# Rows of four later modulation vectors summed on TensorE, three row tiles side by side in column groups

## The chip, the cores and the metric

The kernel runs on one core of one Trainium2 chip. The metric is the device time of one execution in microseconds. Three executions of the kernel before took 723.62, 726.33 and 727.22 us, so its median is 726.33 us. One more execution was taken with the hardware profiler, and every row shown below is from that one.

## The reference

The reference is a decoder trunk of two layers over one sequence of 512 positions and 1024 features. Each layer draws a shift, a scale and a gate from one conditioning vector and computes, in float32:

```python
cond = jax.nn.silu(c)                                   # (1, 1024)
for layer in range(2):
    shift, scale, gate = jnp.split(cond @ w_ada[layer] + b_ada[layer], 3, axis=-1)
    h = x * (1.0 + scale[:, None, :]) + shift[:, None, :]
    y = _even_mixer(h, ...) if layer % 2 == 0 else _odd_mixer(h, ...)
    x = _layer_norm(ALPHA * x + (1.0 + gate[:, None, :]) * y, ln_g[layer], ln_b[layer])
```

The even mixer is one input projection, block-sparse attention over eight heads, sliding-window attention over eight more, a gate and an output projection. The odd mixer is a sparse attention with an indexer and a stick-breaking attention. What the change touches is the product of `cond` with `w_ada` alone: a vector of 1024 times a matrix of 1024 by 1024, once for each of the six pieces (shift, scale and gate of two layers).

## The kernel before, in words

Shift and scale of the first layer are needed at once and are made in `start` by `ada_chunk` (line 519), which is not changed. The other four pieces are "later": the gate of layer 0 and the scale, shift and gate of layer 1. Each is a matrix of 1024 by 1024, that is eight row tiles of 128 rows (index `k`), each in two halves of 512 columns (index `c`). `ada_rows` (line 436) makes 16 steps of a piece, one for each `k` and `c`. A step fetches 128 rows by 512 columns (256 KB) through SyncE's queue into a buffer with the tag `arow` (three buffers while the pool `tmp0` is open, two afterwards), and adds the rows, each multiplied by its element of `cond`, into a tile `accr` of 128 by 1024. On VectorE that is one instruction; on GpSimd it is a multiplication on ScalarE (line 461) and an addition in two halves on GpSimd (line 68, in the helper `Pieces`). The gate of layer 0 gives its first half to VectorE and its second to GpSimd; scale and shift of layer 1 the other way round; the gate of layer 1 gives both to GpSimd. When all rows are in, `column` (line 480) adds up the 128 partitions of `accr` with eight matmuls against a column of ones, and `finish` adds the bias.

Where these steps stand is set by `weave`. It takes a list of attention units, one a turn, spreads the projection's matmuls (`fill`) between their stages, and puts the next of the `side` steps behind every turn. TensorE runs in exactly this written order. The order of the queues of VectorE, ScalarE, GpSimd and SyncE is made by a planner from its own estimate of the times, and each of them works strictly in its order. The side steps go to:

- `attend(0)`, 16 units: six empty steps, then the 21 steps of the gate of layer 0 (16 rows, four empty, one column step);
- `attend(1)`, 16 units: the scale of layer 1 (16 rows, six empty, one column step) and the first half of the shift's rows, 31 steps;
- the first six window units: the remaining 15 steps of the shift, and one of `out_split`;
- the six empty units behind the last window, in which the output projection runs: the 16 row steps of the gate of layer 1. Its column step follows after the first projections of layer 1.

Two constants come from `constants` (line 159): `condr`, which is `cond` repeated 32 times for each `k` (128 by 8 by 32), and `third`, a column with a one in the partitions 0, 32 and 64 and zeros elsewhere. `ada_chunk` uses both: its function `shift` multiplies four row tiles of 256 columns by `condr` on TensorE (line 548), where row tile `k` goes to output partitions `32 * (k % 3)` and up, so that three matmuls write different groups of 32 columns of the array; `third` then adds the three groups.

Of the kernel before, what the change touches and what calls it, by code (L numbers as in the profile page):

```python
# [9 lines left out]
F32 = mybir.dt.float32  # L10
F32R = mybir.dt.float32r
BF = mybir.dt.bfloat16
AF = mybir.ActivationFunctionType
OP = mybir.AluOpType
# [5 lines left out]
DM = 1024  # L20
KT = 8
# [55 lines left out]
class Trunk:  # L77
# [84 lines left out]
    def constants(self):  # L162
        nc, sb, a = self.nc, self.base, self.a
        crow = self.t("rx")[0:8, 0:128]
        nc.sync.dma_start(crow, a["c"].rearrange("o (k p) -> (o k) p", p=128))
        self.ident = sb.tile([128, 128], F32, name="ident")
        nc.sync.dma_start(self.ident, a["k_ident"])
        self.rot = sb.tile([128, 128], F32, name="rot")
        self.ones = sb.tile([128, 128], F32, name="ones")
        nc.vector.memset(self.ones, 1.0)  # L170
        self.eps = sb.tile([128, 1], F32, name="eps")
        nc.vector.memset(self.eps, EPS)
        ps = self.psum("pv", "colc")
        nc.tensor.transpose(ps[:, 0:8], crow, self.ident[0:8, 0:8])
        cc = self.sm("cc", 8)
        nc.vector.tensor_copy(cc, ps[:, 0:8])
        th = self.sm("cth", 8)
        nc.scalar.activation(th, cc, AF.Tanh, scale=0.5)
        nc.vector.tensor_scalar(th, th, 0.5, 0.5, op0=OP.mult, op1=OP.add)
        self.cond = sb.tile([128, 8], F32, name="cond")  # L180
        nc.vector.tensor_tensor(self.cond, th, cc, op=OP.mult)
        self.condr = self.t("r1")[:, 0:256].rearrange("p (k m) -> p k m", m=32)
        nc.vector.tensor_copy(self.condr, self.cond[:, :, None].to_broadcast([128, 8, 32]))
        self.third = self.tmp.tile([128, 1], F32, name="third")
        nc.vector.memset(self.third, 0.0)
        for j in range(3):
            nc.vector.memset(self.third[32 * j:32 * j + 1], 1.0)
# [245 lines left out]
        nc.vector.tensor_tensor(v[:, j, :, 64:128], p4, f32(v[:, j, :, 0:64]), op=OP.subtract)  # L433


    def ada_rows(self, l, part, engines):

        nc = self.nc
        box = {}
        per = 4 if "tmp1" in self.pools else 1  # L440

        def step(k, c):
            cc = slice(512 * c, 512 * c + 512)
            if k % per == 0:
                if per == 1:
                    r = self.ada_row("wr").rearrange("p (a n) -> p a n", a=1)
                else:
                    r = self.base.tile([128, 4, 512], F32, tag="raw", name="wr", bufs=2)
                src = self.a["w_ada"][l][128 * k:128 * (k + per), part * DM + 512 * c:part * DM + 512 * c + 512]
                nc.sync.dma_start(r, src.rearrange("(k p) n -> p k n", p=128))  # L450
                box["r"] = r
                if k + c == 0:
                    box["acc"] = self.base.tile([128, DM], F32, tag="accr", name=f"accr{l}{part}")
            acc, r = box["acc"], box["r"][:, k % per]
            w = self.cond[:, k:k + 1]
            eng = engines[c]
            if eng is self.gp:
                if k == 0:
                    nc.scalar.activation(acc[:, cc], r, AF.Copy, scale=w)
                else:  # L460
                    nc.scalar.activation(r, r, AF.Copy, scale=w)  # L461
                    eng.tensor_tensor(acc[:, cc], acc[:, cc], r, op=OP.add)
            elif k == 0:
                eng.tensor_scalar(acc[:, cc], r, w, None, op0=OP.mult)
            else:
                eng.scalar_tensor_tensor(acc[:, cc], r, w, acc[:, cc], op0=OP.mult, op1=OP.add)  # L466
        steps = [lambda k=k + j, c=c: step(k, c) for k in range(0, KT, per) for c in range(2) for j in range(per)]
        return steps, lambda: box["acc"]

    def ada_row(self, name):  # L470
        return self.tmp.tile([128, 512], F32, tag="arow", name=name, bufs=3 if "tmp0" in self.pools else 2)

    def ada_cols(self, l, parts, engines=None, late=6):


        nc = self.nc
        names = ("shift", "scale", "gate")
        dst = {p: self.base.tile([128, 8], F32, name=f"{names[p]}{l}") for p in parts}

        def column(part, acc, k):  # L480
            if k == 0:
                dst["ps"] = self.psum("pv", f"adac{l}{part}")
            nc.tensor.matmul(dst["ps"][:, k:k + 1], acc[:, k * 128:k * 128 + 128], self.ones[:, 0:1], start=True, stop=True)

        def finish(part):
            ps = dst.pop("ps")
            b0 = 8 + 24 * l + 8 * part
            nc.vector.scalar_tensor_tensor(dst[part], ps[:, 0:8], float(part > 0), self.cols[:, b0:b0 + 8],
                                           op0=OP.add, op1=OP.add)
            if part == 2:  # L490
                nc.vector.tensor_scalar(dst[part], dst[part], 0.5, None, op0=OP.mult)
        steps = []
        for p in parts:
            st, acc = self.ada_rows(l, p, engines or [self.E(z) for z in {0: 'vg', 1: 'gv'}[l]])
            steps += st + [lambda: None] * late
            steps.append(lambda p=p, acc=acc: ([column(p, acc(), k) for k in range(KT)], finish(p)) and None)
        return steps, dst

# [544 lines left out]
    def even_mixer(self, side, more):  # L1043

        nc, W = self.nc, self.a["w_in_even"][0]
# [44 lines left out]
        def bv_turn():  # L1090
            pt = self.psum("pt", "bvT", (128, 4, 128))
            for j in range(QT):
# [6 lines left out]

        fill = [*rotated("aq1", 256, "q1", 0.125, raw), *rotated("ak1", 768, "k1", 1.0), *self.values(W, 1280, "av1", keep("v1")),  # L1100
                self.col_tile(wkv, 0, "bk", bk), self.col_tile(wkv, 1, "bv", bv)]
        self.weave(attend(0), fill, [lambda: None] * 6 + side)
        bq0 = rotated("bq0", 1536, "bq0", 0.125)
        fill = [bq0[0], self.part(bv_turn, 0.43), bq0[1], *rotated("bq1", 1792, "bq1", 0.125), *self.gates(W, 2304, 2, osum[2]),
                *self.gates(W, 2304, 3, osum[3])]
# [340 lines left out]
    def run(self):  # L1446
# [7 lines left out]
        self.at = self.pool("at0")  # L1454
        self.tmp = self.pool("tmp0")
        self.constants()
        side, gate = self.ada_cols(0, (2,), late=4)
        more, ada1 = self.ada_cols(1, (1, 0), late=6)
        steps = side + more
        n0, n1, n2 = 21, 52, 69  # L1460
        osum, window = self.even_mixer(steps[:n0], steps[n0:n1])
        self.close("tmp0")
        self.tmp = self.pool("out0")
        W = self.a["w_in_even"][0]
# [9 lines left out]
        windows = [window(i, g) for i in range(QT) for g in range(2)]  # L1474
        us, box = {}, {}
        o = [f() for f in osum]
        rest = steps[n1:n2]
        self.weave(windows[:6], fill, rest + [lambda: None] * max(0, 5 - len(rest)) + [lambda: self.out_split(0, o, box, (0,))])
        G = to_all()
        self.weave(windows[6:7], [], [lambda n=n: self.out_split(0, o, box, (n,)) for n in (1, 2, 3)])  # L1480

# [11 lines left out]
        fill = self.out_half(0, 0, box, G, resid, done)  # L1493
        self.weave(windows[7:] + [None] * 2, fill[:6])
        self.out_split(1, o, box)
        side, gate1 = self.ada_cols(1, (2,), [self.E(z) for z in 'gg'], 0)
        self.weave([None] * 6, fill[6:], steps[n2:] + side[:-1])
        modulation()
        self.close("qk0")
        h1 = self.pool("h1", side="right")  # L1500
# [23 lines left out]
        first = firsts(halves[0], {})  # L1524
        t = turn(2)
        self.run_parts(*first[2:], self.between(first[0], t[:4]), self.between(first[1], t[4:]))
        for f in side[-1]() or []:
            f()
        self.close("out0", "at0", "h0")

        self.qk_pool = self.pool("x1", side="right")
# [36 lines left out]
        box = {}  # L1568
# [80 lines left out]
```

## Time and profile before

| | kernel before |
|---|---|
| median of three executions | 726.33 us |
| profiled execution | 727.53 us |
| its span, first to last instruction | 725.0 us |
| TensorE matmul (PE) busy | 667.3 us, 92% |
| TensorE weight load (PEld) busy | 539.5 us, 74% |
| VectorE (DVE) busy | 512.7 us, 71% |
| GpSimd (POOL) busy | 381.3 us, 53% |
| ScalarE (ACT) busy | 377.7 us, 52% |
| mean granted TensorE clock | 0.960 |

The profiled execution took 727.53 us, 2.5 us more than its span; it lies 1.2 us above the median of the runs shown. Busy time is the union of an engine's instructions. Matmuls overlap each other in the array, so what TensorE can still take on is better read from the distance between the starts of its instructions than from the busy share. The granted clock is 1 at 2.4 GHz and 0.5 at 1.2 GHz. An "idle before" in square brackets is time in which the engine had nothing to do, with what ended it.

### The profile page before, as it was taken

The numbers are of one execution on the slowest core, as the hardware profiler recorded it, in microseconds if no ns is written. First come the engines' busy times: TensorE is split into PE (matmuls) and PEld (weight loads), VectorE is DVE, ScalarE is ACT, GpSimd is POOL, SyncE is SP. The second block draws the span as 40 slices with busy tenths as digits, with TensorE's granted clock in tenths as the row PEclk, the third lists the DMA queues.
The fourth block names the chain that finished last, engine by engine and source line by source line (L and its number), as shares of the span: only waits on it lengthen the run. The fifth ranks groups of instructions, "written<-read, shape, count | busy, mean of one in ns | idle before, by whom it ended". The sixth has DMA issues, their size and how long they took to land.

```text
span 725.0 us, 11339 instructions
## 1 busy us (share of the span) xinstructions
PE 667.3 (92%) x3866; PEld 539.5 (74%) x3866; DVE 512.7 (71%) x1157; ACT 377.7 (52%) x820; POOL 381.3 (53%) x492
## 2 busy tenths in 40 slices
PE   3799989998999999999999999899999987888994
PEld 1566758875777777799987768687767866777994
DVE  3646376566656888977753269999948979567787
ACT  2225266566555566766523453656656447376630
POOL 1456584135514544696855644445677276361743
PEclk9899999999999998899999999989999999898998
DMA  8991552135315711348443212211167686243231
GB/s 259 345 315 60 175 165 84 55 99 165 117 59 189 258 62 58 106 106 286 149 140 101 73 59 74 62 56 54 34 172 189 169 283 202 67 149 124 86 119 58
DMA packets 82643, 97.55 MB, mean 135 GB/s; under 512 B 8697, under 2 KB 66906, under 8 KB 82586
## 3 DMA queue, kind: packets, MB, share of 16 engines
q1 hardware_dynamic: 82586, 96.84, 43.2%
q8 instruction: 30, 0.49, 0.3%
q14 instruction: 27, 0.22, 0.1%
HBM read 86.32 MB, written 10.49 MB: 134 GB/s over the span
## 4 chain that ended last, share of the span: by engine, by line
PE 55%; DVE 13%; DMA 11%; POOL 10%; ACT 4%; issue 4%; SPq 2%; POOLq 0%; DVEq 0%; ACTq 0%
DMA wr<-in_w_ada 5%; PE gp L306 4%; PE gp L308 4%; PE gp L307 4%; PE s L788 3%; PE pt L712 3%; DMA x<-in_x 2%; PE pv L738 2%; DMA kc<-knh 2%; PE pv L737 2%; PE s L1003 1%; POOL u L68 1%; PE rot L620 1%; POOL accr L68 1%; PE dq L306 1%
## 5 line engine op out<-in xcount | busy, mean ns | idle before, releaser
L68 POOL TENSOR_TENSOR accr<-accr,wr 128x256 f32<-128x256 f32 x70 | 57.6, 846 | 48.8 <-ACT wr L461 45.8
L306 PE MATMUL gp<-hh,gh 128*128 128x512 f32 x128 | 56.9, 445 | 0.0
L714 DVE TENSOR_TENSOR PT<-pt,PT 128x128 fp32r<-128x128 f32 (+1 forms) x96 | 46.3, 482 | 15.0 <-ACT PT L713 13.7
L713 ACT CAST PT<-pt 128x128 fp32r<-128x128 f32 (+1 forms) x96 | 40.6, 423 | 29.7 <-PE pt L712 26.4
L308 PE MATMUL gp<-hh,gl 128*128 128x512 f32 x128 | 51.4, 401 | 0.0
L307 PE MATMUL gp<-hl,gh 128*128 128x512 f32 x128 | 51.3, 401 | 0.0
L68 POOL TENSOR_TENSOR u<-u,gb 128x256 f32<-128x256 f32 (+1 forms) x40 | 32.5, 842 | 25.1 <-ACT u L1584 20.4
L68 POOL TENSOR_TENSOR gl<-g,gh 128x256 fp32r<-128x256 f32 x32 | 25.0, 808 | 34.9 <-ACT gh L271 32.7
L461 ACT ACTIVATE wr<-wr,cond 128x512 f32<-128x512 f32 x35 | 24.8, 720 | 32.9 <-DMA wr<-in_w_ada 31.9
L68 POOL TENSOR_TENSOR o<-o,join 64x256 f32<-64x256 f32 (+1 forms) x26 | 20.2, 777 | 37.1 <-DVE join L767 22.7
L712 PE MATMUL pt<-ident,P 128*128 128x128 f32 x160 | 29.2, 281 | 5.4 <-DVE PT L714 3.8
L1281 DVE TENSOR_TENSOR_SCAN keep<-keep 128x128 f32<-128x128 f32 (+3 forms) x32 | 30.0, 938 | 4.8 <-ACT keep L1280 4.8
L68 POOL TENSOR_TENSOR beta<-beta,keep 128x192 f32<-128x192 f32 (+3 forms) x32 | 19.5, 629 | 22.9 <-DVE keep L1281 22.8
L466 DVE SCALAR_TENSOR_TENSOR accr<-wr,cond,accr 128x512 f32<-128x512 f32 x21 | 19.3, 919 | 16.8 <-DMA wr<-in_w_ada 16.7
L308 PEld LDWEIGHTS gp<-hh,gl 128*128 128x128 f32 x128 | 24.6, 192 | 5.9
L306 PEld LDWEIGHTS gp<-hh,gh 128*128 128x128 f32 x128 | 25.2, 197 | 5.1 <-issue 1.7
L712 PEld LDWEIGHTS pt<-ident,P 128*128 128x128 f32 x160 | 20.2, 143 | 10.3 <-DVE PT L714 4.0
L68 POOL TENSOR_TENSOR hl<-P,hh 128x256 fp32r<-128x256 f32 x28 | 21.9, 810 | 10.9 <-DVE hh L586 10.9
L762 ACT COPY join<-pv 64x256 f32<-64x256 f32 x48 | 17.6, 366 | 18.8 <-PE pv L738 18.2
L307 PEld LDWEIGHTS gp<-hl,gh 128*128 128x128 f32 x128 | 24.9, 195 | 2.8 <-issue 0.2
L1279 ACT ACTIVATE beta<-s 128x128 f32<-128x128 f32 (+3 forms) x32 | 14.0, 439 | 21.6 <-PE s L1277 21.5
L1227 DVE MAX8 m<-wk 128x8 f32<-128x256 f32 (+2 forms) x45 | 24.8, 552 | 0.6
(535 smaller groups left out, 2573.2 us busy)
## 6 DMA issues: line engine op xcount, KB each, us to landing
wr<-in_w_ada SPq DMA_DIRECT2D x64, 256.0 KB
wo<-in_w_out SPq DMA_DIRECT2D x12, 1024.0 KB
wa<-in_w_ada SPq DMA_DIRECT2D x10, 512.0 KB
g<-in_w_in_even SPq DMA_DIRECT2D x4, 1024.0 KB
g<-in_w_in_odd SPq DMA_DIRECT2D x4, 1024.0 KB
wa<-in_w_ada SPq DMA_DIRECT2D x12, 256.0 KB
x<-in_x SPq DMA_DIRECT2D x4, 512.0 KB
aqk<-in_w_in_even SPq DMA_DIRECT2D x4, 512.0 KB
```

Source lines behind the costliest of these rows:

```text
L68: self.eng.tensor_tensor(out, a, b, op=op)
L306: nc.tensor.matmul(ps, w.hi(k)[:, c], self.hh[k][:, q], start=k == 0, stop=False)
L307: nc.tensor.matmul(ps, w.hi(k)[:, c], self.hl[k][:, q], start=False, stop=False)
L308: nc.tensor.matmul(ps, w.lo(k)[:, c], self.hh[k][:, q], start=False, stop=k == KT - 1)
L461: nc.scalar.activation(r, r, AF.Copy, scale=w)
L466: eng.scalar_tensor_tensor(acc[:, cc], r, w, acc[:, cc], op0=OP.mult, op1=OP.add)
L712: nc.tensor.transpose(pt[:, b, :], p[:, b * 128:b * 128 + 128], self.ident)
L713: nc.scalar.copy(hi, pt[:, :nb])
L714: nc.vector.tensor_tensor(lo, pt[:, :nb], f32(hi), op=OP.subtract)
L788: self.nc.tensor.matmul(s, q[a][r, m, c], k[b][r, m, 0:n], start=z == 0, stop=stop and z == 2)
L1227: nc.vector.max(m8, cur)
L1281: nc.vector.tensor_tensor_scan(kp[:, ::-1], kp[:, ::-1], kp[:, ::-1], 1.0, OP.mult, OP.bypass)
```

## The change

The four later pieces are summed on TensorE. `ada_rows` now makes six groups a piece: for each half `c` the row tiles 0 to 2, 3 to 5 and 6 to 7. A group's `load` fetches its two or three tiles of 256 KB into the `arow` buffers, of which there are three in every stage now. Its `use` multiplies each by its 32 columns of `condr`, into partitions 0, 32 and 64 of one PSUM tile with the tag `pv` (two buffers, shared with the attention outputs), and ScalarE copies the first group's result into `accr`, or VectorE adds a later one to it. One step is the use of a group and then the load of the next, so seven steps and a column step make a piece. The column step multiplies 96 partitions by `third`. `condr` and `third` move to a pool that stays open longer.

The steps are placed anew: the gate of layer 0 stays in `attend(0)` (five empty steps, then its eight steps, over 16 turns); scale and shift of layer 1 both go to `attend(1)` (16 steps over 16 turns); the gate of layer 1, with its column step, goes to the first six window units, nine steps over six turns with the one of `out_split`. The six empty units behind the windows have no side steps any more.

```diff
-        self.condr = self.t("r1")[:, 0:256].rearrange("p (k m) -> p k m", m=32)
+        self.condr = self.at.tile([128, 8, 32], F32, name="condr")
-        self.third = self.tmp.tile([128, 1], F32, name="third")
+        self.third = self.at.tile([128, 1], F32, name="third")
...
-    def ada_rows(self, l, part, engines):
+    def ada_rows(self, l, part):
...
-            if eng is self.gp:
-                if k == 0:
-                    nc.scalar.activation(acc[:, cc], r, AF.Copy, scale=w)
-                else:
-                    nc.scalar.activation(r, r, AF.Copy, scale=w)
-                    eng.tensor_tensor(acc[:, cc], acc[:, cc], r, op=OP.add)
-            elif k == 0:
-                eng.tensor_scalar(acc[:, cc], r, w, None, op0=OP.mult)
+        turns = [(c, k) for c in range(2) for k in (0, 3, 6)]
+
+        def load(n):
+            c, k0 = turns[n]
+            box["r"] = [self.ada_row("wr") for _ in range(k0, min(k0 + 3, KT))]
+            for j, r in enumerate(box["r"]):
+                nc.sync.dma_start(r, self.a["w_ada"][l][128 * (k0 + j):128 * (k0 + j) + 128,
+                                                        part * DM + 512 * c:part * DM + 512 * c + 512])
+
+        def use(n):
+            c, k0 = turns[n]
+            if n == 0:
+                box["acc"] = self.base.tile([128, DM], F32, tag="accr", name=f"accr{l}{part}")
+            rows = slice(0, 32 * len(box["r"]))
+            ps, acc = self.psum("pv", "wrs"), box["acc"][rows, 512 * c:512 * c + 512]
+            for j, r in enumerate(box["r"]):
+                nc.tensor.matmul(ps[32 * j:32 * j + 32], self.condr[:, k0 + j], r, start=True, stop=True)
+            if k0 == 0:
+                nc.scalar.copy(acc, ps[rows])
             else:
-                eng.scalar_tensor_tensor(acc[:, cc], r, w, acc[:, cc], op0=OP.mult, op1=OP.add)
-        steps = [lambda k=k + j, c=c: step(k, c) for k in range(0, KT, per) for c in range(2) for j in range(per)]
-        return steps, lambda: box["acc"]
+                nc.vector.tensor_tensor(acc, ps[rows], acc, op=OP.add)
+
+        def step(n):
+            if n:
+                use(n - 1)
+            if n < len(turns):
+                load(n)
+        return [lambda n=n: step(n) for n in range(len(turns) + 1)], lambda: box["acc"]
...
-        return self.tmp.tile([128, 512], F32, tag="arow", name=name, bufs=3 if "tmp0" in self.pools else 2)
+        return self.tmp.tile([128, 512], F32, tag="arow", name=name, bufs=3)
...
-            nc.tensor.matmul(dst["ps"][:, k:k + 1], acc[:, k * 128:k * 128 + 128], self.ones[:, 0:1], start=True, stop=True)
+            nc.tensor.matmul(dst["ps"][:, k:k + 1], acc[0:96, k * 128:k * 128 + 128], self.third[0:96], start=True, stop=True)
...
-        self.weave(attend(0), fill, [lambda: None] * 6 + side)
+        self.weave(attend(0), fill, [lambda: None] * 5 + side)
...
-        side, gate = self.ada_cols(0, (2,), late=4)
-        more, ada1 = self.ada_cols(1, (1, 0), late=6)
-        steps = side + more
-        n0, n1, n2 = 21, 52, 69
-        osum, window = self.even_mixer(steps[:n0], steps[n0:n1])
+        side, gate = self.ada_cols(0, (2,))
+        more, ada1 = self.ada_cols(1, (1, 0))
+        osum, window = self.even_mixer(side, more)
...
-        rest = steps[n1:n2]
-        self.weave(windows[:6], fill, rest + [lambda: None] * max(0, 5 - len(rest)) + [lambda: self.out_split(0, o, box, (0,))])
+        rest, gate1 = self.ada_cols(1, (2,))
+        self.weave(windows[:6], fill, rest + [lambda: self.out_split(0, o, box, (0,))])
...
-        side, gate1 = self.ada_cols(1, (2,), [self.E(z) for z in 'gg'], 0)
-        self.weave([None] * 6, fill[6:], steps[n2:] + side[:-1])
+        self.weave([None] * 6, fill[6:])
...
-        for f in side[-1]() or []:
-            f()
```

## Rows read from the trace of the kernel before

**Rows 1.** Table by stretch: length, busy (count) by engine, granted clock, DMA share, GB/s

```profile
core 0: us, PE busy (x) PEld busy (x) DVE busy (x) ACT busy (x) POOL busy (x), PEclk, DMA share, GB/s
...
110.00:285.00 175.00, 172.05 (x903) 132.08 (x902) 119.18 (x294) 103.49 (x251) 70.35 (x91) 0.99 0.35 113
62.00:372.00 310.00, 300.11 (x1748) 243.79 (x1748) 216.74 (x499) 181.59 (x400) 174.19 (x219) 0.97 0.42 133
372.00:725.00 353.00, 322.91 (x1891) 265.98 (x1890) 265.73 (x591) 179.04 (x393) 183.59 (x234) 0.95 0.37 109
```

**Rows 2.** Timeline of PE, projection: start us, us, what, shapes

```profile
80.18 0.39 PE L306 MATMUL aq<-hh,aq1h 128*128 128x512 f32 x1
80.41 0.39 PE L307 MATMUL aq<-hl,aq1h 128*128 128x512 f32 x1
```

**Rows 3.** Timeline of PE, first of two long waits, idle time in brackets

```profile
101.49 2.08 PE L620 MATMUL rot<-rx,rot 128*128 128x512 f32 x2 [2.97 <-ACT rx L616]
```

**Rows 4.** Table by stretch, at the lower granted clock

```profile
101.06:104.48 3.42, 2.99 (x5) 1.76 (x6) 1.84 (x3) 2.01 (x6) 3.42 (x4) 0.50 0.48 153
...
285.38:292.21 6.83, 6.35 (x22) 4.55 (x21) 6.61 (x14) 4.07 (x10) 5.50 (x8) 0.50 0.27 83
...
295.62:299.04 3.42, 3.42 (x18) 3.42 (x18) 3.42 (x9) 3.14 (x9) 3.00 (x4) 0.50 0.01 5
```

**Rows 5.** Table by stretch, the last window units and the output projection

```profile
285.00:312.00 27.00, 25.26 (x149) 21.70 (x150) 23.78 (x60) 19.67 (x48) 20.13 (x26) 0.81 0.32 99
312.00:350.00 38.00, 36.46 (x287) 34.56 (x286) 30.39 (x61) 22.17 (x36) 30.32 (x39) 1.00 0.65 200
```

**Rows 6.** Timeline of PE around one four-tile product with condr

```profile
41.14 0.39 PE L308 MATMUL ak<-hh,ak0l 128*128 128x512 f32 x1
41.45 1.05 PE L548 MATMUL shift<-wa,r 128*32 128x256 f32 x8
42.44 0.50 PE L306 MATMUL aq<-hh,aq0h 128*128 128x512 f32 x1
42.78 0.40 PE L307 MATMUL aq<-hl,aq0h 128*128 128x512 f32 x1
```

**Rows 7.** Line 548 in slices of 0.05 us: length, PE busy (instructions in flight)

```profile
41.45:41.50 0.05, 0.05 (x3) 1.00 1.12 369
...
41.70:41.75 0.05, 0.05 (x6) 1.00 0.93 277
```

**Rows 8.** Costliest groups, the row sums: busy us, mean ns, idle before, releaser

```profile
L68 POOL TENSOR_TENSOR accr<-accr,wr 128x256 f32<-128x256 f32 x70 | 57.6, 846 | 48.8 <-ACT wr L461 45.8
...
L466 DVE SCALAR_TENSOR_TENSOR accr<-wr,cond,accr 128x512 f32<-128x512 f32 x21 | 19.3, 919 | 16.8 <-DMA wr<-in_w_ada 16.7
```

**Rows 9.** Reads of a PSUM tile of 128x512: ns min/median/max, first and last start

```profile
L624 DVE TENSOR_TENSOR r<-rot,sin x13: 671/686/694, 64.7 to 201.3; 128x512 f32<-128x512 f32 x13
...
L616 ACT ACTIVATE rx<-aq x4: 572/587/599, 59.0 to 100.8; 128x512 f32<-128x512 f32 x4
```

**Rows 10.** Timeline of PE, first score matmul of four units of attend(1)

```profile
189.93 0.44 PE L788 MATMUL s<-ak1h,aq1h 64*128 64x384 f32 x1
...
211.81 0.50 PE L788 MATMUL s<-ak1h,aq1h 64*128 64x512 f32 x1
...
218.53 0.32 PE L788 MATMUL s<-ak1h,aq1h 64*128 64x128 f32 x1
...
221.62 0.39 PE L788 MATMUL s<-ak1h,aq1h 64*128 64x256 f32 x1
```

**Rows 11.** Chain that ended last: start us, us, what; three fetches

```profile
90.57 2.67 DMA wr<-in_w_ada
...
161.73 5.98 DMA wr<-in_w_ada
...
170.56 3.00 DMA wr<-in_w_ada
```

**Rows 12.** Table by stretch, the fetches of start

```profile
26.00:56.00 30.00, 30.00 (x162) 20.46 (x160) 15.98 (x31) 8.97 (x17) 14.70 (x22) 0.94 0.97 308
```

**Rows 13.** SyncE's waits, 60 to 372 us: total us, times, longest us

```profile
SPq L246 <- DVE bq0l L275: 15.2, 1, 15.2
```

More of the change, by code (lines that the diff above doesn't have):

```diff
@@ L433, in v_split @@
         nc.vector.tensor_tensor(v[:, j, :, 64:128], p4, f32(v[:, j, :, 0:64]), op=OP.subtract)
-    def ada_rows(self, l, part, engines):
+    def ada_rows(self, l, part):
         nc = self.nc
         box = {}
[L440 to L446, printed above, removed]
-                else:
[L448 to L456, printed above, removed]
-            if eng is self.gp:
-                if k == 0:
-                    nc.scalar.activation(acc[:, cc], r, AF.Copy, scale=w)
-                else:
-                    nc.scalar.activation(r, r, AF.Copy, scale=w)
-                    eng.tensor_tensor(acc[:, cc], acc[:, cc], r, op=OP.add)
-            elif k == 0:
-                eng.tensor_scalar(acc[:, cc], r, w, None, op0=OP.mult)
-            else:
-                eng.scalar_tensor_tensor(acc[:, cc], r, w, acc[:, cc], op0=OP.mult, op1=OP.add)
-        steps = [lambda k=k + j, c=c: step(k, c) for k in range(0, KT, per) for c in range(2) for j in range(per)]
-        return steps, lambda: box["acc"]
@@ L470, in ada_row, with ada_cols @@
+        def step(n):
[4 more added lines that the diff above has]
+        return [lambda n=n: step(n) for n in range(len(turns) + 1)], lambda: box["acc"]
     def ada_row(self, name):
-        return self.tmp.tile([128, 512], F32, tag="arow", name=name, bufs=3 if "tmp0" in self.pools else 2)
-    def ada_cols(self, l, parts, engines=None, late=6):
+        return self.tmp.tile([128, 512], F32, tag="arow", name=name, bufs=3)
+    def ada_cols(self, l, parts):
@@ L493, in ada_cols @@
         for p in parts:
-            st, acc = self.ada_rows(l, p, engines or [self.E(z) for z in {0: 'vg', 1: 'gv'}[l]])
-            steps += st + [lambda: None] * late
+            st, acc = self.ada_rows(l, p)
+            steps += st
             steps.append(lambda p=p, acc=acc: ([column(p, acc(), k) for k in range(KT)], finish(p)) and None)
```

## The prediction

> **What bounds the kernel now.** I read the table by stretch first. The later modulation is made between 62 and 372 us. In these 310 us TensorE is busy for 300.1, and idle for 9.9 [rows 1]. VectorE has 93 us to spare there and GpSimd 136, so what is taken from them is worth something only where TensorE waits for them. Busy is not the same as full, so I looked at the timeline next: a matmul over 512 columns follows the one before it by 0.23 us (80.18 to 80.41) [rows 2], and 512 columns at 2.4 GHz last 0.21 us. The projection runs at the rate of its columns: **TensorE is full**, and what is put on it there pushes the end out by its own length. I then looked for the idle time that can be won. There are two waits of about 3 us each (2.97 and 2.95) for an eviction on ScalarE [rows 3]; the chain leads from there back through VectorE and ScalarE to the fetches of the rows, for which VectorE, working in order, stood still. Behind each wait the clock is granted at half for 3.4 us, and it is at half twice more behind the window units, for 6.8 and 3.4 us [rows 4]. At half clock TensorE does half its work, so 1.7 + 1.7 + 3.4 + 1.7 = 8.5 us go that way. **All that can be won** between 62 and 372 us is therefore 9.9 + 8.5 = 18.4 us.
>
> **What the change takes away.** GpSimd's 57.6 us of additions and VectorE's 19.3 us, with the multiplications on ScalarE ahead of GpSimd's [rows 8]. Of that the path sees the waits alone. The two waits near 100 and 178 us should go, since no row sum stands in VectorE's queue for a fetch any more: 2.97 + 2.95 + 2 x 1.7 = 9.3 us. In the stretch of the last windows and the output projection TensorE is idle for 1.7 + 1.5 = 3.3 us [rows 5] and loses 5.1 us to the half clock [rows 4]. There the 16 row steps of the last gate leave GpSimd, but the weight splits and the window's softmax stay. I count half of these 8.4 us, 4.2; the bounds are 0 and 8.4. Together **-13.5 us**, with 18.4 as the most.
>
> **What it adds on TensorE.** Four pieces of six groups are 24 uses; 16 of them have three row tiles and eight have two. The nearest row is the product with `condr` in `start`: four tiles of 256 columns. Three matmuls are in flight within the first 0.05 us and six after 0.25 [rows 7], so the three column groups do run side by side. That stretch lies between two projection matmuls, 41.14 to 42.78; less 2 x 0.23 for the two projection matmuls at its ends it costs 1.64 - 0.46 = 1.18 us [rows 2, 6]. Four tiles in three groups are two rounds over 256 columns; a group of the new kind is one round over 512, which is the same number of columns. I take 1.18 us a use, for two tiles as for three: 24 x 1.18 = **+28.3 us**. The lower bound is that the switch at both ends is hidden, 0.99 us each (41.45 to 42.44), 23.8 in all. The upper one is that the groups do not overlap (a rival, below). Nothing hides this, since the stretch from 110 to 285 us, where most uses go, has 2.95 us of idle time in all [rows 1], and that is the second of the waits counted above. The column steps keep their eight matmuls, on 96 partitions instead of 128: nothing.
>
> **What it adds elsewhere.** 16 additions from PSUM on VectorE at 0.69 us and eight copies on ScalarE at 0.59 [rows 9], 11 and 4.7 us. VectorE is busy for 119 of the 175 us between 110 and 285 [rows 1] and gives up more than it gets; nothing, as long as that room is there. Without it 15.7 us is the most. These additions wait for TensorE, and behind them in VectorE's order stand the softmax steps of the next units, which TensorE needs a full turn later; a short wait of theirs is covered by that turn.
>
> **The waits that it adds.** A load takes the three buffers which the use just ahead of it gives back, and the next use comes one step later. So each fetch of three tiles must land within one turn. One fetch of 256 KB, with nothing beside it, takes 2.67 us from issue to release [rows 11]. Two more are 0.52 MB, and at 308 GB/s, with the DMA engines at 97% [rows 12], that is 1.7 us. My estimate for three tiles is 4.4 us. A turn of `attend(1)` lasts (211.81 - 189.93) / 5 = 4.38 us without the new use [rows 10]: **it just fits**, and in the mean nothing is left over. The shortest turn is 3.1 us (218.53 to 221.62) [rows 10], 1.3 short; I count 2.7 us for it and three others that are a little short. A fetch behind a weight load of 1 MB took 5.98 us where it otherwise took 3.00 [rows 11]; I count one such hit, 3.0. The loads also stand in SyncE's queue, with the weight loads behind them, and SyncE once stood for 15.2 us before a weight load until a buffer was free [rows 13]; a load behind that would be late, which belongs to the upper bound. So **+5.7 us** in the attentions, between 0 and 43 (15 uses that are bound to the turn before, each 2.9 us late, as if a weight load stood ahead of every one).
>
> In the window units nine steps fall on six turns, 1, 2, 1, 2, 1, 2. In the second and fourth turn a use, the load behind it and the use of that load follow each other directly on TensorE, with no other matmul between. There the whole fetch is waited for: 2 x 4.4 = **+8.8 us**. After waits of 3 us the clock was at half for 3.4 us [rows 3, 4], so these two cost 2 x 1.7 = **+3.4 us** more. The window unit that takes two `arow` buffers for its probabilities gets one of them only when the last group has been used, at the end of its turn; the scores of the next unit cover that, nothing.
>
> **The sum.** 28.3 + 5.7 + 8.8 + 3.4 - 13.5 = +32.7 us. The profiled execution took 727.53 us, and would take 760; on the median of the runs, 726.33, it is **759 us**.
>
> **The rivals.**
> *Faster: TensorE still has room.* In the table by stretch the weight loads fill only 132 of the 175 us between 110 and 285 [rows 1]. If the 43 us left were room for more matmuls, the uses would cost nothing, since they need 28.3. Then 12.2 us of waits for the doubled steps and their clock stand against 18.4 us won, -6.2, and 720 us. It decides from the point at which the uses cost less than 6 us in all. Against it stands the distance of 0.23 us between the starts, which leaves no room [rows 2]. The Trainium skill (Trainium Kernel Development and Optimization, Performance Expectations) calls matmul busy time a bad metric of how close a kernel is to its limit and names the busy share of weight loads a good one; by that rule it would come out as this rival says. The distance between the starts speaks against it here. Chance 0.05, of which 0.01 falls within 0.5% (3.6 us, about what a measurement of this kernel can tell from no change).
> *Cheap: the loads land in time.* No wait in the attentions and all 18.4 us won: 28.3 + 12.2 - 18.4 = +22.1, 748 us; with the lower price of a use 744. For it: 4.4 against 4.38 us is no clear wait. Chance 0.17, of which 0.02 comes within 0.5% where the doubled steps should cost nothing either.
> *Dear: the loads are the bound.* If eight of the 15 uses come 2.9 us late, with half a clock behind each, that is 8 x (2.9 + 1.7) = 36.8 in place of 5.7, 790 us. For it: SyncE's queue in order, with weight loads that hold it. Chance 0.15.
> *The change does not do what it says.* If the column groups ran one after another, a use of three tiles would last 3 x 0.86 + 0.3 = 2.9 us (0.86 being two passes of 0.43, the round of rows 6 at twice its columns and half its number), one of two tiles 2.0: 16 x 2.9 + 8 x 2.0 = 62.4 in place of 28.3, 793 us. The six matmuls in flight speak against it [rows 7]. Chance 0.03.
>
> **How the numbers follow.** The forecast, +32.7, has 0.60, with 748 to 774 as its own range. The range reaches over the cheap case down to 741 and into the dear one up to 783, which leaves out the faster rival, the groups one after another and most of the dear one: 0.2. Faster by over 0.5%: 0.04; within: 0.03; slower: 0.93.
>
> **What would show it.** In the profile after: the matmuls from `wr` 24 times about 1 us, with the projection around them at the old distances; no idle time of 3 us near 100 and 178 us; two waits of TensorE of about 4 us for `wr` in the window units, each with the clock at half behind it; GpSimd's busy time down by some 58 us, with no gain from it. Wrong would be: a stretch from 110 to 285 us that is not longer by some 20 us (TensorE had room), waits for `wr` in most turns of the attentions (the loads are the bound), or a gain behind 372 us, which I expect to be unchanged.

## The result and the profile after

| | before | after |
|---|---|---|
| median of four executions | 725.74 us | 769.95 us |
| all executions | 723.62 to 727.22 us | 763.10 to 772.01 us |
| profiled execution, its span | 727.53, 725.0 us | 763.10, 761.3 us |

The changed kernel is slower by a ratio of 1.058 (95% interval 1.053 to 1.062), 44 us. The forecast was 759 us in a range from 741 to 783. The profiled execution of the changed kernel is the fastest of its four: it ran at a mean granted clock of 0.954, the other three at 0.945 to 0.949. The two profiled executions are 35.6 us apart, and these can be followed in the traces. The remaining 8.6 of the 44 us lie between the profiled executions and the medians (the one after is 6.9 us below its median, the one before 1.8 above), and no trace shows where.

The page's busy times, engine by engine, with share of the span and number of instructions:

```profile
PE 699.7 (92%) x3994; PEld 547.0 (72%) x3994; DVE 496.5 (65%) x1149; ACT 358.5 (47%) x788; POOL 319.3 (42%) x422
```

GpSimd does 62 us less, VectorE 16, ScalarE 19, and none of it shortened the kernel. TensorE does 32 us more. To see where, both kernels are cut at two places that they share: the first score matmul of `attend(0)`, and the first product of layer 1 (`small`). This is the table by stretch of the kernel after, with the columns of [rows 1], from the one to the other and from there to the end; below it stands the same cut of the kernel before.

```profile
80.96:391.58 310.62, 301.34 (x1629) 221.88 (x1628) 184.37 (x462) 147.59 (x343) 84.02 (x113) 0.95 0.36 116
391.58:761.30 369.72, 337.45 (x2031) 281.24 (x2029) 271.14 (x606) 186.14 (x405) 197.24 (x254) 0.96 0.39 115
```

```profile
78.89:354.14 275.25, 266.06 (x1484) 212.16 (x1484) 195.79 (x468) 164.67 (x374) 143.89 (x182) 0.97 0.41 131
354.14:725.00 370.86, 340.77 (x2047) 283.84 (x2045) 275.77 (x609) 188.25 (x407) 199.21 (x255) 0.95 0.38 115
```

The stretch with the row sums grew by 35.4 us, from 275.25 to 310.62. What follows it hardly changed (370.86 and 369.72; the last gate's column step, 1.7 us, has left it), and what lies ahead grew by 2.1.

A use in an attention turn, timeline of TensorE (start us, us, what, shapes), answers to [rows 6]:

```profile
139.97 0.40 PE L308 MATMUL bk<-hh,bkvl 128*128 128x512 f32 x1
140.30 1.06 PE L457 MATMUL wrs<-wr,condr 128*32 128x512 f32 x6
141.29 0.38 PE L788 MATMUL s<-ak0h,aq0h 64*128 64x256 f32 x1
```

From its start to the next matmul are 0.99 us. The distance from the projection to it, 0.33 us, is the one that the projection had to a score matmul before as well (189.60 to 189.93 in the trace before), so the switch of the array costs nothing extra there:

```profile
189.60 0.40 PE L308 MATMUL bq<-hh,bq1l 128*128 128x512 f32 x1
```

Four of the 18 uses in the attentions come late. In the latest, the last tile lands behind the first two, and the next matmul starts 2.42 us after the first of the use, not 0.99 (145.71 to 148.13):

```profile
145.71 1.05 PE L457 MATMUL wrs<-wr,condr 128*32 128x512 f32 x4
147.16 1.04 PE L457 MATMUL wrs<-wr,condr 128*32 128x512 f32 x2 [0.40 <-DMA wr<-in_w_ada]
148.13 0.44 PE L788 MATMUL s<-ak0h,aq0h 64*128 64x384 f32 x1
```

The kernel before had its two long waits in the attentions, the first in [rows 3], the second here; the trace after has neither:

```profile
179.89 2.07 PE L620 MATMUL rot<-rx,rot 128*128 128x512 f32 x2 [2.95 <-ACT rx L616]
```

The two doubled steps, that is the two turns of the window units in which a second use stands right behind the first, in the same view:

```profile
269.90 1.06 PE L457 MATMUL wrs<-wr,condr 128*32 128x512 f32 x6
275.87 3.14 PE L457 MATMUL wrs<-wr,condr 128*32 128x512 f32 x6 [4.91 <-DMA wr<-in_w_ada]
278.94 0.58 PE L1003 MATMUL s<-bkh,bq0h 64*128 64x256 f32 x1
...
300.64 1.06 PE L457 MATMUL wrs<-wr,condr 128*32 128x512 f32 x6
304.61 2.83 PE L457 MATMUL wrs<-wr,condr 128*32 128x512 f32 x4 [2.91 <-DMA wr<-in_w_ada]
307.94 1.22 PE L457 MATMUL wrs<-wr,condr 128*32 128x512 f32 x2 [0.50 <-DMA wr<-in_w_ada]
309.09 0.38 PE L1003 MATMUL s<-bkh,bq0h 64*128 64x256 f32 x1
```

When TensorE has used one group, the next is fetched into its buffers, and TensorE does nothing until it lands. The chain that ended last shows the same place, with the fetch behind the use on which it depends (start us, us, what):

```profile
269.97 1.07 PE wrs L457 x6
...
271.06 4.67 DMA wr<-in_w_ada
...
275.87 3.14 PE wrs L457 x6
```

The stretches of the kernel after at the lower granted clock, table by stretch, answer to [rows 4]:

```profile
161.56:164.97 3.41, 3.41 (x11) 2.62 (x10) 0.90 (x3) 0.62 (x3) 2.13 (x4) 0.50 0.09 9
209.35:212.76 3.41, 3.41 (x8) 1.94 (x7) 2.07 (x7) 0.49 (x2) 0.76 (x2) 0.50 0.80 251
253.72:260.55 6.83, 6.83 (x22) 5.27 (x23) 3.65 (x16) 1.69 (x10) 2.42 (x4) 0.50 0.70 253
274.20:287.85 13.65, 11.98 (x32) 7.02 (x33) 4.26 (x15) 2.22 (x10) 0.00 (x0) 0.50 0.31 107
304.92:308.33 3.41, 2.91 (x5) 0.37 (x4) 0.12 (x1) 0.00 (x0) 0.00 (x0) 0.50 0.79 252
332.23:335.64 3.41, 3.30 (x12) 2.41 (x11) 3.41 (x8) 3.04 (x9) 3.41 (x4) 0.50 0.00 0
```

These are 34.1 us at 1.2 GHz, where the kernel before had 17.1: the three stretches of [rows 4] and this one.

```profile
179.57:182.98 3.41, 3.09 (x5) 1.73 (x6) 2.83 (x8) 2.14 (x6) 3.41 (x5) 0.50 0.33 101
```

The fourth stretch after begins in the first wait for a fetch, the fifth 0.3 us behind the end of the second (304.61). The other four begin 2.5 to 5 us behind the starts of the four column steps (158.73, 206.32, 251.21 and 327.32), of which this is one; before, one column step in four was followed by such a stretch.

```profile
158.73 1.84 PE L483 MATMUL adac<-third,accr 96*128 96x1 f32 x16
```

What was forecast, and what the trace shows for the stretch:

| term | forecast | measured |
|---|---|---|
| 24 uses | +28.3 | 24 x 0.98 = +23.5 |
| late fetches in the attentions | +5.7 | +3.6 (four uses of 18, 0.1 to 1.4 each) |
| the two doubled steps | +8.8 | +11.6 |
| idle time won | -7.6 (5.9 for the two waits, half of 3.3 behind) | -8.6 |
| half clock | -2.5 (+3.4 - 3.4 - half of 5.1) | +8.5; some 3 of it fall into waits counted above, an estimate from the sum of these rows, 38.6, against 35.4 |
| sum | +32.7 | +35.4 |

The 11.6 us are the time from 269.90 to 278.94 and from 300.64 to 309.09, 17.5 in all, less four uses of 0.98 us, less 2 us for the two of them that ran at half clock. Idle time won is the 9.2 us without a busy TensorE before (275.25 less 266.06) against 0.6 after: 310.62 less 301.34, less 8.7 that this row of TensorE's waits gives to fetches (total us, times, longest us):

```profile
PE wrs L457 <- DMA wr<-in_w_ada: 8.7, 4, 4.9
```

The half clock is half of 34.1 less half of 17.1 us. In its forecast and in that of the idle time the -13.5 and the +3.4 of the prediction are split into the two.

### The profile page after: what moved, and what is told of

It is laid out like the page before. It is cut to its first block, busy times and chain, and to the rows that moved or that the text cites. A ratio compares the mean times of both kernels' runs of the same rounds, so it can differ in the third digit from the quotient of the medians.

```text
span 761.3 us, 11456 instructions
## 1 busy us (share of the span) xinstructions
PE 699.7 (92%) x3994; PEld 547.0 (72%) x3994; DVE 496.5 (65%) x1149; ACT 358.5 (47%) x788; POOL 319.3 (42%) x422
## 4 chain that ended last, share of the span: by engine, by line
PE 71%; DVE 9%; DMA 8%; POOL 6%; ACT 3%; issue 2%; SPq 2%; POOLq 0%; ACTq 0%; DVEq 0%
PE gp L306 4%; PE s L788 4%; PE gp L307 4%; PE gp L308 4%; PE wrs L457 4%; PE pt L712 3%; PE s L1003 2%; PE y L855 2%; PE y L854 2%; PE y L856 2%; DMA x<-in_x 2%; DMA wr<-in_w_ada 2%; PE pv L738 2%; PE pv L737 2%; PE rot L620 1%
## 5 line engine op out<-in xcount | busy, mean ns | idle before, releaser
L306 PE MATMUL gp<-hh,gh 128*128 128x512 f32 x128 | 59.0, 461 | 0.0
L308 PE MATMUL gp<-hh,gl 128*128 128x512 f32 x128 | 53.2, 416 | 0.0
L307 PE MATMUL gp<-hl,gh 128*128 128x512 f32 x128 | 53.1, 415 | 0.0
L68 POOL TENSOR_TENSOR u<-u,gb 128x256 f32<-128x256 f32 (+1 forms) x40 | 32.7, 846 | 25.4 <-ACT u L1579 20.4
L457 PE MATMUL wrs<-wr,condr 128*32 128x512 f32 x128 | 33.6, 639 | 8.7 <-DMA wr<-in_w_ada 8.7
L796 ACT ACTIVATE P<-P,st 128x128 f32<-128x128 f32 (+3 forms) x32 | 18.0, 563 | 39.2 <-DVE st L795 39.2
L68 POOL TENSOR_TENSOR r<-rx,cos 128x256 f32<-128x256 f32 x26 | 19.0, 752 | 33.9 <-ACT rx L616 26.9
L1013 ACT ACTIVATE P<-s,stw 128x256 f32<-128x256 f32 (+1 forms) x32 | 14.0, 442 | 35.5 <-DVE stw L1008 32.3
L795 DVE CUSTOM_DVE_ANT_0 P<-s,upto 128x128 f32<-128x128 f32 (+3 forms) x32 | 15.6, 489 | 21.0 <-PE s L788 20.7
L712 PEld LDWEIGHTS pt<-ident,P 128*128 128x128 f32 x160 | 20.6, 146 | 11.6 <-DVE PT L714 4.0
L68 POOL TENSOR_TENSOR wo0l<-wo,wo0h 128x256 fp32r<-128x256 f32 x16 | 12.4, 813 | 39.3 <-ACT wo0h L271 39.3
L461 DVE TENSOR_TENSOR accr<-wrs,accr 96x512 f32<-96x512 f32 (+1 forms) x16 | 10.9, 684 | 26.0 <-PE wrs L457 25.9
```

The costliest lines, as they stand in the source:

```text
L68: self.eng.tensor_tensor(out, a, b, op=op)
L306: nc.tensor.matmul(ps, w.hi(k)[:, c], self.hh[k][:, q], start=k == 0, stop=False)
L307: nc.tensor.matmul(ps, w.hi(k)[:, c], self.hl[k][:, q], start=False, stop=False)
L308: nc.tensor.matmul(ps, w.lo(k)[:, c], self.hh[k][:, q], start=False, stop=k == KT - 1)
L457: nc.tensor.matmul(ps[32 * j:32 * j + 32], self.condr[:, k0 + j], r, start=True, stop=True)
L712: nc.tensor.transpose(pt[:, b, :], p[:, b * 128:b * 128 + 128], self.ident)
```

## The experiments

Each kernel was timed beside the kernel before on the same chip, and its ratio is to that one. "The stretch" is the one from the first score matmul to the first product of layer 1.

### The steps spread over the windows

```diff
-        self.weave(windows[:6], fill, rest + [lambda: self.out_split(0, o, box, (0,))])
+        self.weave(windows[:6], fill, [*rest[:3], lambda: None, *rest[3:5], lambda: self.out_split(0, o, box, (0,))])
...
-        self.weave(windows[6:7], [], [lambda n=n: self.out_split(0, o, box, (n,)) for n in (1, 2, 3)])
+        self.weave(windows[6:7], [], [rest[5]] + [lambda n=n: self.out_split(0, o, box, (n,)) for n in (1, 2, 3)])
...
-        self.weave(windows[7:] + [None] * 2, fill[:6])
+        self.weave(windows[7:] + [None] * 2, fill[:6], rest[6:])
```

> The changed kernel with the steps of the last gate set one to a turn: one of them in each window unit, the last two behind the last window, so that no use follows its own load directly. Theory 1 (TensorE is full; on top of the uses the doubled steps cost their fetch, 4.9 and 3.4 us of idle time in the trace after, and the half clock of 13.6 and 3.4 us behind them, which takes 8.5 us): 770 - 8.3 - 8.5 = 753 us, and no half clock of more than 3.5 us in the window units. Theory 2 (the uses themselves, not the waits, let the clock fall): the waits go, the half clock stays, about 762 us.

Measured: 746.82 us, ratio 1.026 (1.020 to 1.031). The table by stretch of this kernel:

```profile
80.92:374.63 293.71, 289.72 (x1628) 215.63 (x1628) 182.25 (x462) 147.32 (x343) 83.41 (x113) 0.99 0.38 123
374.63:745.30 370.67, 340.11 (x2031) 281.43 (x2029) 271.45 (x606) 186.64 (x405) 196.96 (x254) 0.96 0.38 115
251.50:258.33 6.83, 6.83 (x24) 5.27 (x23) 3.31 (x16) 1.69 (x10) 2.16 (x4) 0.50 0.73 251
```

The stretch shrank from 310.62 to 293.71, by 16.9 us where 16.8 were expected. Of the half clock 6.8 us are left, behind one column step. All 24 uses are still there, so it is not the uses that let the clock fall: theory 2 is out. Setting the steps one to a turn won 17 us of the 35.

That it is just the expected size is in part luck. Three of the four stretches at half clock behind column steps went as well, 5.1 us of lost work that theory 1 had not counted. Against that, uses still come late, by 7.4 us in all where those in the attentions of the changed kernel did by 3.6. The latest starts at 304.74, and the next matmul at 308.73, 3.0 us later than it could:

```profile
307.21 1.59 PE L457 MATMUL wrs<-wr,condr 128*32 128x512 f32 x4 [1.43 <-DMA wr<-in_w_ada]
```

### The fetches left out

```diff
         def load(n):
             c, k0 = turns[n]
-            box["r"] = [self.ada_row("wr") for _ in range(k0, min(k0 + 3, KT))]
+            if n:
+                box["r"] = box["all"][:min(k0 + 3, KT) - k0]
+                return
+            box["r"] = box["all"] = [self.ada_row("wr") for _ in range(k0, min(k0 + 3, KT))]
...
```

> The changed kernel with only the first group of each of the four pieces fetched; the other five uses of a piece multiply the same tiles again. The fetches of 52 of the 64 row tiles are left out, so the sums are other sums. All 24 uses stay. Theory 1 (uses plus doubled waits): the 8.3 us of doubled waits, their 8.5 us of half clock and the 3.4 us of waits in the attentions go, 770 - 20 = 750 us, some 3 us below the kernel with the steps spread. Rival (the loads in SyncE's queue hold the weight loads behind them, and that is the bound): far below it, 735 us or less.

Measured: 747.23 us, ratio 1.026 (1.021 to 1.031), the same as with the steps spread. Every use in the attentions lasts 0.98 or 0.99 us here. With no fetch to wait for the kernel is still 20 us behind the one before: the loads in SyncE's queue are not the bound. That it comes out level with the spread steps does not mean that fetches cost nothing there. The 7.4 us of late uses are gone, but the stretch has 20.5 us at half clock in place of 6.8: three pieces of 3.4 us behind column steps, and one of 10.2 that begins in a wait of the score matmuls for probabilities. The stretch, the longest of the four pieces and that wait (total us, times, longest us):

```profile
81.17:376.01 294.84, 290.07 (x1629) 219.07 (x1628) 184.39 (x462) 147.59 (x343) 83.73 (x113) 0.97 0.24 76
315.58:325.82 10.24, 9.66 (x39) 8.09 (x40) 7.35 (x27) 4.79 (x21) 0.00 (x0) 0.50 0.10 33
```

```profile
PE s L1006 <- ACT P L1016: 3.1, 1, 3.1
```

### One column group

```diff
-            rows = slice(0, 32 * len(box["r"]))
+            rows, last = slice(0, 32), len(box["r"]) - 1
...
-                nc.tensor.matmul(ps[32 * j:32 * j + 32], self.condr[:, k0 + j], r, start=True, stop=True)
+                nc.tensor.matmul(ps[0:32], self.condr[:, k0 + j], r, start=j == 0, stop=j == last)
...
```

> The changed kernel with all tiles of a use in the same 32 columns of the array, added up in one PSUM tile of 32 partitions, so that they can't run side by side. Theory 1 (three column groups run at the same time): 16 uses of three tiles last 1.73 us longer and eight of two tiles 0.86 us, +34.6, 770 + 35 = 805 us. Rival (the groups bring nothing, since the matmuls of a use run one after another anyway): 770 us.

Measured: 798.46 us, ratio 1.096 (1.092 to 1.101). The timeline of TensorE shows the use itself:

```profile
179.27 0.40 PE L308 MATMUL bq<-hh,bq0l 128*128 128x512 f32 x1
179.59 2.76 PE L457 MATMUL wrs<-wr,condr 128*32 128x512 f32 x6
182.28 0.44 PE L788 MATMUL s<-ak1h,aq1h 64*128 64x384 f32 x1
```

2.69 us against 0.99: three tiles side by side cost little more than a third of three in a row. The column step adds up 32 partitions here in place of 96. The stretch grew from 310.62 to 343.19, by 32.6 us where 34.6 were expected. The rival that the groups bring nothing is out.

This trace also shows a wait of 2.9 us for a fetch that no half clock follows: behind it the granted clock stays at 1.00.

```profile
81.32:424.51 343.19, 330.77 (x1629) 229.98 (x1629) 184.29 (x462) 147.86 (x343) 83.61 (x113) 0.95 0.33 105
296.71:303.00 6.29, 6.29 (x25) 3.17 (x26) 1.99 (x4) 0.99 (x4) 0.00 (x0) 1.00 0.44 140
```

```profile
296.71 2.73 PE L457 MATMUL wrs<-wr,condr 128*32 128x512 f32 x6 [2.91 <-DMA wr<-in_w_ada]
```

### No row sums at all, from the kernel before

```diff
         def step(k, c):
-            ...
+            if k + c == 0:
+                box["acc"] = self.base.tile([128, DM], F32, tag="accr", name=f"accr{l}{part}")
+                nc.gpsimd.memset(box["acc"], 0.0)
...
```

> The kernel before with the row sums of the four later pieces left out, fetches and all: the sum tile is set to zero by GpSimd instead. The column steps stay. It shows what the row sums cost before. Theory 1 (they cost the two waits of 3 us and a part of the half clock and the idle time, 13.5 us, 18.4 at most): 726 - 13.5 = 712 us, not under 707. Rival (VectorE and GpSimd paced more of the kernel than the idle time of TensorE shows): under 700 us.

Measured: 718.23 us, ratio 0.987 (0.982 to 0.991). The table by stretch, and the waits of TensorE in the stretch (total us, times, longest us):

```profile
80.90:346.10 265.20, 262.63 (x1484) 212.04 (x1484) 171.53 (x444) 142.04 (x335) 87.22 (x116) 0.97 0.23 73
...
278.66:295.73 17.07, 14.86 (x57) 11.65 (x56) 12.98 (x41) 8.72 (x29) 6.87 (x10) 0.50 0.18 61
```

```profile
PE s L982 <- ACT P L992: 2.2, 2, 1.5
```

The whole of the row sums cost the kernel before 9.3 us (727.50 on that chip less 718.23; 6 to 13 by the interval of the ratio); 13.5 were expected and 18.4 held for the most. The stretch of this trace is 10.1 us shorter than before (265.20 against 275.25). The two waits of 3 us are gone. The half clock is not: 17.1 us of it, as before, now in one piece around the last windows, with no row sum in the kernel.

### Half the columns

```diff
-            ps, acc = self.psum("pv", "wrs"), box["acc"][rows, 512 * c:512 * c + 512]
+            ps, acc = self.psum("pv", "wrs"), box["acc"][rows, 512 * c:512 * c + 256]
+            ps = ps[:, 0:256]
...
-                nc.tensor.matmul(ps[32 * j:32 * j + 32], self.condr[:, k0 + j], r, start=True, stop=True)
+                nc.tensor.matmul(ps[32 * j:32 * j + 32], self.condr[:, k0 + j], r[:, 0:256], start=True, stop=True)
```

This is on top of the spread steps; the sum tile is set to zero first, since half of it is no longer written.

> The kernel with the spread steps, where each use multiplies and adds only 256 of its 512 columns; all tiles are still fetched whole. Half of the columns of the four sums are left out. Theory 1 (TensorE is full, and a use is paid by its columns): a use falls from 0.98 to 0.55 us, 24 x 0.43 = 10.3 us less, 747 - 10 = 737 us. Rival (a use is paid as a step, by the switch of the array, its PSUM buffer and the additions behind it): 744 us or more.

Measured: 740.34 us, ratio 1.019 (1.013 to 1.026). In the timeline a use is 0.56 us long, and the stretch is 281.18, 12.5 less than with all columns:

```profile
168.51 0.63 PE L459 MATMUL wrs<-wr,condr 128*32 128x256 f32 x6
169.07 0.44 PE L790 MATMUL s<-ak1h,aq1h 64*128 64x384 f32 x1
```

```profile
81.34:362.52 281.18, 278.16 (x1628) 215.46 (x1628) 177.85 (x462) 145.96 (x343) 86.57 (x116) 0.99 0.39 128
362.52:738.90 376.38, 342.24 (x2031) 284.53 (x2029) 274.79 (x606) 187.06 (x405) 195.42 (x254) 0.94 0.37 113
```

In the stretch the 10.3 us that the columns are worth come back, and 2 more; uses come late by about 1 us less, and a wait of 1.8 us for probabilities behind one use is gone. In the total only 6.5 do: the part behind, in which no edit lies, took 376.38 us here and 370.67 with the spread steps, at a mean granted clock of 0.94 against 0.96. The total alone would have left this open between the two expectations; the stretch says that a use is paid by its columns.

### Wide column steps

A column step's 16 one-column matmuls were made 64 columns wide in the changed kernel, in the one with the spread steps and in the kernel before:

```diff
-            nc.tensor.matmul(dst["ps"][:, k:k + 1], acc[0:96, k * 128:k * 128 + 128], self.third[0:96], start=True, stop=True)
+            nc.tensor.matmul(dst["ps"][:, 64 * k:64 * k + 64], acc[0:96, k * 128:k * 128 + 128], self.ones[0:96, 0:64], start=True, stop=True)
...
```

> The changed kernel with the 16 one-column matmuls of a column step made 64 columns wide (against a block of ones, with the factor 1/32 for the 32 equal rows put into condr), so that TensorE works on many columns in these 1.77 us. Theory 1 (the clock goes to half behind a column step since nearly nothing passes through the array in it; in the trace after all four are followed by a half clock, of 3.4, 3.4, 6.8 and 3.4 us, 8.5 us of lost work): these four stretches go, 770 - 8.5 = 761 us; those behind the doubled steps stay. Rival (the half clock has another cause, the uses or the wait for the last addition): 770 us, and half clocks behind the column steps as before.

> The spread steps and the wide column steps together. Theory 1: the kernel with the spread steps has one half clock of 6.8 us behind a column step left; without it 747 - 3.4 = 743 us, which is 718 us of the kernel without row sums plus 24 uses of 0.98 us (23.5 us) and some 2 us of fetches that come late: the uses alone keep it slower than the kernel before. Rival (there is still a gain of over 10 us hidden behind the clock): 735 us or less.

> The kernel before with the column steps 64 columns wide, nothing else. Theory 1 (clock behind the column steps): one of the four was followed by a half clock, of 6.8 us, in the trace of before; without it 727 - 3.4 = 723 us or a little more, since the output projection behind it has other waits. Rival (the clock there fell for another reason, as the waits for probabilities of the last windows): 727 us and the half clock near 285 us still there.

Measured: 767.16 us, ratio 1.053 (1.045 to 1.060), for the changed kernel; 751.99 us, 1.034 (1.027 to 1.041), with the spread steps; 727.15 us, 1.002 (0.999 to 1.005), for the kernel before. None is a gain. With the spread steps it looks like this:

```profile
79.70:370.00 290.30, 287.49 (x1629) 214.88 (x1629) 182.42 (x462) 147.11 (x343) 83.86 (x113) 0.99 0.38 124
370.00:748.90 378.90, 344.10 (x2031) 286.73 (x2028) 276.89 (x606) 186.42 (x405) 195.98 (x254) 0.94 0.37 112
```

The stretch is 3.4 us shorter than with thin column steps (293.71), and in this trace and that of the kernel before with wide steps no half clock follows a column step within 6 us. But the part behind took 378.90 us in place of 370.67, and the medians do not improve. In the changed kernel with wide steps, whose profiled execution is the slowest of its four (770.84 us), one column step in four is followed by a half clock all the same, 3.3 us behind its start at 247.39. The stretch and that half clock:

```profile
79.70:393.30 313.60, 301.42 (x1629) 222.29 (x1629) 183.57 (x462) 147.69 (x343) 84.65 (x113) 0.95 0.35 114
250.69:257.52 6.83, 6.83 (x22) 5.40 (x22) 2.29 (x13) 2.07 (x11) 1.64 (x3) 0.50 0.68 229
```

Over all traces of this case a half clock began within 5 us of the start of 15 of 36 thin column steps (four of four in the changed kernel, one of four with the steps spread and before, none of four with the sums on GpSimd), and of 1 of 12 wide ones. That the thin column steps let the clock fall remains likely, not shown, and making them wide does not always keep it up.

### The sums on one engine, from the kernel before

In `ada_cols`, the engines of the first three pieces; in the first kernel all four pieces then run on ScalarE and GpSimd, in the second three run on VectorE:

```diff
-            st, acc = self.ada_rows(l, p, engines or [self.E(z) for z in {0: 'vg', 1: 'gv'}[l]])
+            st, acc = self.ada_rows(l, p, engines or [self.E(z) for z in 'gg'])
```

```diff
-            st, acc = self.ada_rows(l, p, engines or [self.E(z) for z in {0: 'vg', 1: 'gv'}[l]])
+            st, acc = self.ada_rows(l, p, engines or [self.E(z) for z in 'vv'])
```

> The kernel before with all row sums on ScalarE and GpSimd, none on VectorE. The step tested is that the two waits of 3 us near 100 and 178 us come from VectorE standing still for the fetches. Theory 1: both go, and with them 9.3 us of idle time and half clock; of the kernel without row sums (718 us) some 2 us stay: 720 us. Rival (ScalarE, which works in order too and then multiplies all 64 tiles, 46 us, holds the evictions just as long, and GpSimd with 109 us of additions delays weight splits): 727 us or more.

> The kernel before with the row sums of the first three later pieces all on VectorE, so that ScalarE neither waits for their fetches nor multiplies them; the last gate stays on ScalarE and GpSimd. With the sums all on ScalarE and GpSimd the two waits of 3 us for an eviction on ScalarE stayed. Theory A (ScalarE, working in order, is the one that stood still): the two waits go, 720 us. Theory B (whichever engine carries the sums stands still for the fetches and passes it on): the waits stay, 726 us or more.

Measured: 736.07 us, ratio 1.013 (1.008 to 1.018), with GpSimd; 728.93 us, 1.004 (1.001 to 1.007), with VectorE. The waits of TensorE for the eviction, first with GpSimd, then with VectorE:

```profile
PE rot L620 <- ACT rx L616: 5.4, 3, 2.7
```

```profile
PE rot L620 <- ACT rx L616: 2.5, 1, 2.5
```

With no row sum on VectorE both waits stay; with none of the three pieces on ScalarE the second goes and the first stays. Theory 1 and theory A are both out. Theory B holds for the first wait: in the chain that ends there, the engine that stands still for a fetch and passes the delay on is ScalarE in the one kernel (97.73, `wr` L461, behind a fetch of 2.61 us) and VectorE in the other (94.62, `accr` L466, behind one of 2.82).

```profile
97.73 0.72 ACT wr L461
```

```profile
94.62 0.75 DVE accr L466
```

For the second wait it does not hold; why that one went with the sums on VectorE stays open.

No kernel here is faster than the one before with the sums in it. By the kernel without sums, a better way to make them could win some 9.3 us, 2.3 us a piece. On TensorE a piece costs 6 x 0.98 = 5.9 us; to break even a use would have to be shorter than 0.4 us.

## Why the prediction was right, and where it was off

**TensorE is full: right.** All 24 uses appear at full length in the stretch, and halving their columns or putting them in a row moves the stretch by the columns (12.5 less for 10.3, 32.6 more for 34.6). The rival that TensorE still has room is out. The Trainium skill (Trainium Kernel Development and Optimization, Performance Expectations) names the busy share of weight loads as one of two good metrics of how close a kernel is to its limit; this one does not hold here: weight loads filled 132 of 175 us [rows 1], and there was no room.

**The price of a use: 1.18 us taken, 0.98 measured**, the lower bound of the text (0.99). The mis-sized part is the switch at both ends. In the row that I took it from, the product stands between two projection matmuls [rows 6]; in the new places it stands between the projection and a score matmul, where the distance was 0.33 us already.

**The waits in the attentions: 5.7 us taken, 3.6 measured.** That a fetch just fits into a turn was right: 14 of the 18 uses there did not come late. **The doubled steps: right in place, 8.8 taken, 11.6 measured**; the first fetch took 4.67 us from issue to release where 4.4 were estimated, and the use behind each wait ran for the most part at half clock; in the second its last tile was still on the way (307.94).

**The half clock is the step that failed.** I took two things for granted: that the half clock behind the two old waits would go with them, and that only the two doubled steps would bring new ones, of 3.4 us each. The first did happen; but the wait of 4.9 us brought 13.7 us at half clock, not 3.4, and all four column steps were followed by such a stretch. Net +8.5 us in place of -2.5. A wait of a given length did not bring a half clock of a given length either: of two waits of 2.9 us for a fetch, one was followed by 3.4 us (changed kernel) and one by none (one column group). The same error stands in the bound of 18.4 us for all that can be won: without any row sums the kernel still spends 17.1 us at half clock in the stretch, so leaving the sums out won back none of the 8.5 us that the bound counts for it.

**That the sum came out near is in part luck.** The uses were 4.8 us cheaper than forecast, the late fetches 2.1, and the idle time gave 1.0 more; that stands against 2.8 us for the doubled steps and the miss on the half clock. On the medians the forecast of 759 us is 11 us low, 8.6 of them the part that no trace shows.

**Where the waits come from: half right.** Both vanished, as forecast, but not since VectorE was freed: with VectorE free and the sums on ScalarE and GpSimd they stay. In the changed kernel and in the one without row sums, where neither VectorE nor ScalarE waits for a fetch of rows, both are gone.

**The offloaded work: right.** GpSimd's busy time fell by 62 us and VectorE's by 16, and the kernel did not notice.

## What to carry to other kernels

Before work is moved onto an engine, measure the distance between the starts of its instructions in the place where it will go: where that is the time of their columns already, the move costs its full length, and what can come back is small (here leaving the old work out altogether won 9 us, against 23.5 for the new). Tiles side by side in column groups are worth having (0.99 against 2.69 us for three), but only for work that has to be on TensorE anyway. A load that is "one step ahead" is ahead only where other work lies between the steps: count the steps for each turn, since two on one turn put the whole fetch on the path.

## What the runs showed that was not expected

The part behind the stretch moves the total by about as much as some of the changes do, and most of that goes with the granted clock. It took 370.67 us with the spread steps, 376.38 with half the columns and 378.90 with wide column steps, though no edit of these kernels lies in it. These traces have 33, 44 and 43 us at half clock there, which is some 5 us of lost work more in the last two. But the code there is not quite the same: the planner put VectorE's 606 instructions into another order in the last two kernels (163 places differ). Where the order is that of the spread steps, the part took 369.29 us (fetches left out), 372.09 (one column group) and 375.80 (the changed kernel with wide column steps, its slowest execution). Whether the order or chance lets the clock fall there is not shown. An edit that is worth a few us should be read from its own stretch and not from the total alone.
